# A decoder trunk on one core: Q/K outputs in three steps, class copies of K ahead of the exponentials, and stores and loads on other queues

## The chip, the core and the metric

The kernel runs on one core of a Trainium2 chip. The core has a matrix engine (TensorE, PE in the profile, with its weight loads as PEld), a vector engine (VectorE, DVE), a scalar engine (ScalarE, ACT), GpSimd (POOL) and a sync engine (SyncE, SP) that here only issues transfers. DVE, ACT, POOL and SP each work through their own instructions in the order of the program, so an instruction that waits holds up all that stands behind it on its engine. Transfers can be issued by SP, ACT and POOL; the issuing engine waits first for what the transfer needs. Sums of matmuls land in eight banks of PSUM. The metric is the device time of one execution in microseconds, as the median of several runs.

## What is computed

A two-layer decoder trunk over 1024 positions with a residual stream of width 1024, in float32. Layer 0 mixes with a short gated convolution, layer 1 with dilated attention; a SwiGLU network follows each. The change touches the attention layer alone. Its mixer, cut to what matters:

```
qkv = (h @ w_qkv).reshape(bsz, seq, 3, 16, 64)
for window, dilation in ((128, 1), (512, 4), (2048, 16)):
    # query t attends to keys t - j*dilation, j = 0..window//dilation
    s   = q.k / 8 + rel_bias[t5_bucket(distance)]     # masked outside the band
    lse = logsumexp(s);  o = exp(s - lse) @ v
alpha = softmax over the three branches of lse
o = sum(alpha * o) ;  x = x + o.reshape(seq, 1024) @ w_out
```

So a head's result is one weighted sum over all keys of its three branches, divided by one common sum of exponentials.

## The kernel before

All matrix products are made of float32 parts: an operand is split into a rounded high part, copied by ACT (line 141), and the low rest, subtracted by DVE (line 142), and each product is three matmuls (high by high, high by low, low by high). Large products use Strassen's scheme with seven products for a 2x2 block. The order of everything is written out by hand as Python generators that are stepped in turn; each step issues a few instructions, and the order of issue is the order on each engine.

**The Q/K phase.** `QueryKey.mix` (line 1142) makes Q and K of the first six pairs of heads: 42 products in `products` (588), each with `whole` (602), which may save a bank to SBUF on ACT (566, tile `part`) and add others on DVE (570). Each finished quarter of an output goes to `out`, which queues a generator in `waiting`. After each product `filled` calls `idle`, which steps that queue. One output (`emit`, 1124) is scaled by DVE (1128 for K, which also reorders it in time, 1130 for Q), split into high and low parts (tiles `kq_hi` and `kq_lo`), and both are stored to DRAM on POOL's queue (1135, 1136). Pairs 6 and 7 are made later by `projections` (1462) as filler in the attention.

**The attention.** Sixteen heads, two to a pair, p = n // 2 and a = n % 2. `slot(n)` (1710) issues the period of head n, in two loops of eight.

The first loop makes the logits of head n (`scores`, 1531) and the value products of head n - 1 (`values`, 1610) by turns. The logits of the branch with dilation 4 use `kca`, a copy of K ordered by residue class that ACT makes (`classes`, 1524, line 1528); the others use `ka` as loaded. DVE adds the bias (1555, 1564, 1581, 1586) and takes the maximum over the branches (up to 1595); POOL takes it over the partitions (1598, the all-reduce). At the end of the values ACT copies the numerators `o` and the denominators `z` out of PSUM (1640, 1641).

The second loop issues the softmax: five subtractions on DVE (1606), each followed by its exponential on ACT (1607), for the tiles `lf`, `lh`, `ld`, `lp` (two pieces); then, in its steps 5 and 6, the class copies of the next head.

Both loops also step the filler, `fill` (1802): the values V of later heads (`value_tiles`, 1478: lines 1489 to 1491, eviction 1494 on ACT, four stores to `vdram` per tile, 1498 on SP's queue), Q and K of pairs 6 and 7, and from head 12 on the first part of the output projection. A period has 15 steps of it (20 from head 13); a step is mostly six matmuls of 128x256 or three of 128x512. Without `late` the first loop takes one at its steps 0, 2, 4 and 6, and a period of an even head one more ahead of its logits; the second loop spreads what is left. Weights for the filler are loaded on SP (155) and split when `take` asks for the one ahead.

Transfers of a period: at its start bias, K and Q of the next head, on SP (1439, 1440 and 1518 to 1522); in even periods, between the loops, V of the pair into `vx` (`load_values`, 1501: six loads on ACT's queue, 1506 and 1508, which wait until PE has finished the pair before). Even periods also `finish` the pair before (1644): `z` is stored to DRAM (1649), loaded back as a thin tile `zc` (1652), inverted by DVE (1654), stored (1655) and loaded again as a broadcast over the partitions (1657), all four on SP's queue. The next odd period multiplies `o` by it on DVE (1704) and stores the result on POOL's queue (1705). For the last pair this runs on POOL's queue (1665, 1667, 1693, 1695).

Of the kernel before, what the change touches and what calls it, by code (L numbers as in the profile page):

```python
# [97 lines left out]
def trunk(ctx: ExitStack, tc: tile.TileContext, x, gains_in, cwi, ck, cwo, wqkv, wo, relb,  # L98
# [19 lines left out]
    def half(h):  # L118
        return slice(h * HALF, (h + 1) * HALF)
# [990 lines left out]
    class QueryKey(Conv):  # L1110


        def __init__(self, norm):
            Strassen.__init__(self, QK, norm, QK_PAIRS, 0, 1, 0, None)
            self.waiting, self.ready = [], False
            self.kq = {(p, part): dram.tile([256, S], F32, name=f"kq{p}_{part}")
                       for p in range(NPAIR) for part in range(2)}

# [5 lines left out]
        def emit(self, p, part, h, v):  # L1124

            t, rstd = half_page("kq"), self.norm.rstd[:, half(h)]
            if part == 1:
                nc.vector.tensor_tensor(out=by_time(t), in0=by_residue(v), in1=by_residue(rstd), op=ALU.mult)
            else:
                nc.vector.scalar_tensor_tensor(t, v, 0.125, rstd, op0=ALU.mult, op1=ALU.mult)  # L1130
            yield 1
            to = self.kq[p, part]
            hi, lo = half_page("kq_hi", F32R), half_page("kq_lo", F32R)
            split(t, (hi, lo))
            nc.gpsimd.dma_start(to[:128, half(h)], hi.bitcast(F32))
            nc.gpsimd.dma_start(to[128:, half(h)], lo.bitcast(F32))
            yield 1

        def work(self, u, c, v):
            yield from self.emit(u, 1 - c[0], c[1], v)  # L1140

        def mix(self):
            norm = self.norm
            prep = self.differences()
            stats = norm.stats(0, S)
            x12 = []

            def start(n):
                if n == 0:
                    next(prep)  # L1150
                    ensure(self.at(2, 2))
                elif n == 1:
                    next(prep)
                elif n == 3:
                    self.first(0)
                    ensure(self.at(4, 1))
                elif n == 4:
                    self.first(1)
                    ensure(self.at(4, 2))
                elif n == 5:  # L1160
                    ensure(self.at(0, 6))
                elif n == 6:
                    ensure(self.at(1, 6))
                elif n == 7:
                    next(prep)
                elif n == 8:
                    self.first(2)
                    ensure(self.at(0, 7))
                elif n == 9:
                    next(prep)  # L1170
                    next(prep)
                elif n in (10, 12):
                    next(prep)
                elif n == 11:
                    next(prep)
                    self.first(3)
                elif n == 13:
                    self.first(4)
                elif n == 14:
                    next(prep, None)  # L1180
                elif n == 20:
                    self.ahead = 3

            def gather():
                next(stats)

            def spread():
                run(stats)
                self.ready = True

            def load():
                for k in range(4):
                    x12.append(half_page("x12"))
                    nc.sync.dma_start(x12[k], spill[k][:, half(1)])

            def last_operand():
                self.b[8] = [None] * 4
                for k in range(4):
                    self.operand(8, k, k, x12[k])

            def filled(n):
                start(n)
                self.idle(n)

            norm.flush()
            self.base = op_state[1]
            ensure(self.at(0, 2))
            self.products(filled, {(1, 2): gather, (3, 1): spread, (5, 1): load, (5, 7): last_operand})
            self.h = [[self.b[1 + 7 * h * (k < 4) + (1 + h) * (k > 3)][k % 4] for k in range(KT)] for h in range(2)]
            self.step(None)  # L1210


    class Swiglu(Strassen):
# [239 lines left out]
    def attention(norm, qk):  # L1453
# [7 lines left out]

        def projections(p):

            late = []
            for part in (1, 0):
                w = take(("qkv", p, part), 2 - part)
                for h in range(2):
                    b = bank()
                    for _ in product(w, range(KT), qk.h[h], {HALVES[0]: b}):
                        if late and next(late[0], None) is None:  # L1470
                            late.pop()
                        yield
                    late.append(qk.emit(p, part, h, b))
                    next(late[0])
                    yield
            run(*late)

        def value_tiles(g, j):

            if j == 0:  # L1480
                wv[:] = [take(("v", g, i), 1) for i in range(2)]
            v = page("v")
            for b4 in range(4):
                t = 4 * j + b4
                b = bank()[:, :256]
                for k in range(KT):
                    (hi, lo), (whi, wlo) = qk.h[j][k], wv[k // 4]
                    a, c = slice(b4 * 128, b4 * 128 + 128), slice(k % 4 * 256, k % 4 * 256 + 256)
                    nc.tensor.matmul(b, hi[:, a], whi[:, c], start=k == 0, stop=False)  # L1489
                    nc.tensor.matmul(b, hi[:, a], wlo[:, c], start=False, stop=False)  # L1490
                    nc.tensor.matmul(b, lo[:, a], whi[:, c], start=False, stop=k == KT - 1)
                    if k % 2:
                        yield
                nc.scalar.activation(v[:, b4 * 256:b4 * 256 + 256], b, AF.Identity, scale=norm.r[:, t:t + 1])
                yield
            vd = vdram[g]
            for r in range(4):
                nc.sync.dma_start(bass.AP(vd.tensor, vd.offset + (512 * j + r) * 256,
                                          [[16 * 256, 32], [4 * 256, 4], [1, 256]]), v[32 * r:32 * r + 32])

        def load_values(p):
            src = vdram[p // 2]
            for a in range(2):
                off = src.offset + p % 2 * 128 + a * 64
                dims = slice(128 * a, 128 * a + 64)
                nc.scalar.dma_start(vx[:, 0:8, dims], bass.AP(src.tensor, off, [[256, 128], [128 * 256, 8], [1, 64]]))
                for h in range(2):
                    nc.scalar.dma_start(vx[:, 8 + 4 * h:12 + 4 * h, dims],
                                        bass.AP(src.tensor, off + 512 * 256 * h, [[1024, 128], [256, 4], [1, 64]]))

        def load_kq(n):
# [132 lines left out]
        def finish(p):  # L1644

            o, z = OZ.pop(p)
            if p < NPAIR - 1:
                zd, rd = zdram[p]
                nc.sync.dma_start(zd, z[0:65:64])
                yield  # L1650
                zc = scope["pool"].tile([128, 16], F32, name="zc", tag="zc", bufs=2)
                nc.sync.dma_start(zc, bass.AP(zd.tensor, zd.offset, [[16, 128], [1, 16]]))
                yield
                nc.vector.reciprocal(zc, zc)
                nc.sync.dma_start(bass.AP(rd.tensor, rd.offset, [[16, 128], [1, 16]]), zc)
                yield
                nc.sync.dma_start(z, bass.AP(rd.tensor, rd.offset, [[S, 2], [0, 64], [1, S]]))
                yield
                put_off.append((p, o, z))
                return  # L1660
# [49 lines left out]
        def slot(n, dense, ndense, late=0, hook=iter(())):  # L1710
# [28 lines left out]
            for i in range(8):  # L1739
                next(sc, None)  # L1740
                next(pv, None)
                next(pv, None)
                if i >= late and i % 2 == 0:
                    other(1)
                    used += 1
            run(sc)
# [8 lines left out]
            for i in range(8):  # L1755
                if a == 1 and i == 2:
                    attended()
                if i < FIN0 or i > SOFT:
                    next(extra, None)
                if i > SOFT:  # L1760
                    next(later, None)
                if i == SOFT:
                    if n < H:
                        live[n] = new
                        run(softmax(new))
                if i >= SOFT:
                    next(hook, None)
                other(left * (i + 1) // 8 - left * i // 8)
# [258 lines left out]
```

## Time and profile before

| | us |
|---|---|
| runs | 2250.13, 2250.79, 2255.63 |
| median | 2250.79 |
| profiled execution | 2252.32 |
| its span, first to last instruction | 2250.5 |
| mean granted PE clock | 0.976 |

The profile is of one execution. A row of a group gives line, engine and operation, tiles written and read, count, busy time and mean duration, and then the idle time of the engine just before and what ended it. A row of a stretch gives its limits, its length, and per engine the busy time and the count of instructions, and last the mean granted PE clock, the mean busy share of the 16 DMA engines and GB/s. A wait's releaser is inferred: where several things were waited for, it is the last. Matmuls overlap, so that the starts of two tell more than the duration of one.

### The profile page before, as it was taken

The page shows a single profiled execution, that of the slowest core. Times are in us where ns is not written, and L with a number is a line of the kernel's source. Part 1 is how long each engine was busy: PE and PEld are TensorE (multiplying, and loading weights), DVE is VectorE, ACT ScalarE, POOL GpSimd, SP SyncE. Part 2 cuts the span into 40 slices and gives each one's busy share as a digit, 9 for nine tenths or more (in the row PEclk, how much of TensorE's full clock was granted, in tenths as well). Part 3 has the DMA queues.
Part 4 walks back from the last instruction along what each step waited for, and adds up shares of the span by engine and source line. Part 5 has one row for each costly group of instructions (what it writes and reads, how often), then busy time and mean ns, then how long its engine had stood idle before and what let it go on. Part 6 is the DMA issues. An engine that isn't in the chain of part 4 may idle for free. (4 is left out here: it accounts for less than half of the span.)

```text
span 2250.5 us, 30931 instructions
## 1 busy us (share of the span) xinstructions
PE 2143.5 (95%) x11086; PEld 1834.9 (82%) x11086; DVE 1752.9 (78%) x3272; ACT 1004.3 (45%) x1848; POOL 219.1 (10%) x303
## 2 busy tenths in 40 slices
PE   9999999999999999998978888789999999999998
PEld 7888888888888888776877878678788888888887
DVE  8897679988887889688645564677898888888886
ACT  7333345444444644353333333344644444446435
POOL 1000000110100000002211111111101010101000
PEclk9999999999999999999998899899999999999999
DMA  7222652233333674416465554765422333357532
GB/s 217 89 87 78 213 159 70 89 111 105 107 108 123 201 215 131 148 64 205 171 150 144 132 151 120 206 177 165 112 94 99 104 108 104 108 190 219 174 97 75
DMA packets 147588, 304.91 MB, mean 135 GB/s; under 512 B 50328, under 2 KB 61608, under 8 KB 147434
## 3 DMA queue, kind: packets, MB, share of 16 engines
q1 hardware_dynamic: 81514, 201.59, 29.8%
q0 software_dynamic: 24752, 78.25, 10.7%
q10 hardware_dynamic: 41168, 23.10, 3.4%
q8 instruction: 88, 1.44, 0.3%
q14 instruction: 66, 0.54, 0.1%
HBM read 212.48 MB, written 83.05 MB: 131 GB/s over the span
## 5 line engine op out<-in xcount | busy, mean ns | idle before, releaser
L560 PE MATMUL bank<-b,w 128*128 128x512 f32 x1952 | 766.0, 392 | 7.0 <-ACT part L566 5.3
L562 PE MATMUL bank<-b,w 128*128 128x512 f32 x1952 | 763.1, 391 | 8.9 <-DVE w L142 8.8
L561 PE MATMUL bank<-b,w 128*128 128x512 f32 x1952 | 763.0, 391 | 2.5 <-DVE b L553 2.2
L562 PEld LDWEIGHTS bank<-b,w 128*128 128x128 f32 x1952 | 367.8, 188 | 91.9 <-DVE w L142 15.3
L560 PEld LDWEIGHTS bank<-b,w 128*128 128x128 f32 x1952 | 367.8, 188 | 86.5 <-ACT part L566 6.9
L561 PEld LDWEIGHTS bank<-b,w 128*128 128x128 f32 x1952 | 368.1, 189 | 79.1 <-DVE b L553 3.1
L141 ACT ACTIVATE w<-combo 128x512 fp32r<-128x512 f32 (+2 forms) x488 | 248.9, 540 | 222.1 <-DVE combo L189 205.3
L142 DVE TENSOR_TENSOR w<-combo,w 128x512 fp32r<-128x512 f32 (+2 forms) x488 | 276.1, 579 | 38.0 <-ACT w L141 37.3
L566 ACT ACTIVATE part<-bank 128x512 f32<-128x512 f32 x186 | 110.7, 595 | 384.2 <-PE bank L562 382.3
L142 DVE TENSOR_TENSOR w<-raw,w 128x512 fp32r<-128x512 f32 (+2 forms) x334 | 182.1, 566 | 37.5 <-ACT w L141 37.5
L570 DVE TENSOR_TENSOR part<-part,bank 128x256 f32<-128x256 f32 (+1 forms) x366 | 170.4, 495 | 30.1 <-PE bank L562 16.7
L141 ACT ACTIVATE w<-raw 128x512 fp32r<-128x512 f32 (+2 forms) x334 | 161.2, 525 | 47.6 <-PE bank L562 11.5
L369 PE MATMUL bank<-w_hi,w 128*128 128x512 f32 (+1 forms) x320 | 119.6, 374 | 0.0
L371 PE MATMUL bank<-w_hi,w 128*128 128x512 f32 (+1 forms) x320 | 117.9, 368 | 0.7 <-DVE w L142 0.7
L370 PE MATMUL bank<-w_lo,w 128*128 128x512 f32 (+1 forms) x320 | 117.8, 368 | 0.0
L790 DVE TENSOR_TENSOR x<-x,bank 128x512 f32<-128x512 f32 x136 | 92.5, 680 | 29.2 <-PE bank L562 29.2
L491 DVE TENSOR_TENSOR x<-x,bank 128x512 f32<-128x512 f32 (+1 forms) x104 | 66.3, 642 | 62.4 <-PE bank L371 58.3
L189 DVE TENSOR_TENSOR combo<-raw 128x512 f32<-128x512 f32 (+1 forms) x172 | 111.1, 646 | 0.0
L1544 PE MATMUL bank<-qa,kca 128*128 128x256 f32 (+1 forms) x128 | 40.9, 343 | 60.7 <-ACT kca L1528 60.7
L553 DVE TENSOR_TENSOR b<-hin,b 128x512 fp32r<-128x512 f32 x126 | 79.5, 683 | 9.3 <-ACT b L552 9.0
L1489 PE MATMUL bank<-w_hi,b 128*128 128x256 f32 x256 | 78.4, 306 | 7.6 <-ACT w_hi L141 7.6
L1555 DVE TENSOR_TENSOR lf<-bank,bias 128x256 f32<-128x256 f32 x64 | 24.0, 418 | 77.2 <-PE bank L1545 63.8
(248 smaller groups left out, 3716.3 us busy)
## 6 DMA issues: line engine op xcount, KB each, us to landing
hin<-part SPq DMA_DIRECT2D x126, 256.0 KB
raw<-in_ffn_w_gate SPq DMA_DIRECT2D x44, 512.0 KB
raw<-in_ffn_w_up SPq DMA_DIRECT2D x44, 512.0 KB
part<-sum POOLq DMA_DIRECT2D x72, 256.0 KB, 2.3
raw<-in_ffn_w_down SPq DMA_DIRECT2D x48, 384.0 KB
raw<-in_attn_w_qkv SPq DMA_DIRECT2D x27, 512.0 KB
raw<-in_conv_w_in SPq DMA_DIRECT2D x24, 512.0 KB
part<-part POOLq DMA_DIRECT2D x36, 256.0 KB, 2.4
```

Of the source, the lines that this page charges most:

```text
L141: nc.scalar.activation(hi, src, AF.Copy)
L142: eng.tensor_tensor(out=lo, in0=src, in1=hi, op=ALU.subtract)
L189: eng.tensor_tensor(out=c, in0=a, in1=b, op=op)
L369: nc.tensor.matmul(b, whi[:, a], ahi[:, s], start=first, stop=False)
L370: nc.tensor.matmul(b, whi[:, a], alo[:, s], start=False, stop=False)
L371: nc.tensor.matmul(b, wlo[:, a], ahi[:, s], start=False, stop=last)
L560: nc.tensor.matmul(b, hi[:, a], bhi, start=start and k == 0, stop=False, skip_group_check=True)
L561: nc.tensor.matmul(b, hi[:, a], blo, start=False, stop=False, skip_group_check=True)
L562: nc.tensor.matmul(b, lo[:, a], bhi, start=False, stop=k == n - 1, skip_group_check=True)
L566: nc.scalar.activation(t, b, AF.Copy)
L570: nc.vector.tensor_tensor(out=t, in0=t, in1=b, op=ALU.add)
L790: nc.vector.tensor_tensor(out=X[n][:, half(h)], in0=X[n][:, half(h)], in1=b, op=ALU.add)
```

## The change

- `emit` is in three steps instead of two: DVE scales; ACT copies the high part, which is stored; DVE subtracts the low part, which is stored. `step` now keeps two outputs going: after a product it issues the copy of the output before, the scaling of a new one, and the subtraction of the output before. In `projections` the steps of an output follow one per filler step.
- The class copies of the next head move from steps 5 and 6 of the second loop to steps 1 and 2, ahead of the softmax in step 4.
- The filler of the first loop keeps its steps 0 and 2 and gives up 4 and 6 (except with `late`, head 14); they go to the second loop.
- The four stores of a V tile move from SP's queue to ACT's, the six loads of `vx` from ACT's to SP's.
- The four transfers of `finish` move from SP's queue to POOL's (the last pair is unchanged).

```diff
-            yield 1
-            to = self.kq[p, part]
-            hi, lo = half_page("kq_hi", F32R), half_page("kq_lo", F32R)
-            split(t, (hi, lo))
+            yield
+            hi, lo, to = half_page("kq_hi", F32R), half_page("kq_lo", F32R), self.kq[p, part]
+            nc.scalar.activation(hi, t, AF.Copy)
             nc.gpsimd.dma_start(to[:128, half(h)], hi.bitcast(F32))
+            yield
+            nc.vector.tensor_tensor(out=lo, in0=t, in1=hi, op=ALU.subtract)
             nc.gpsimd.dma_start(to[128:, half(h)], lo.bitcast(F32))
-            yield 1
-
-        def work(self, u, c, v):
-            yield from self.emit(u, 1 - c[0], c[1], v)
+
+        def out(self, u, c, v):
+            self.waiting.append(self.emit(u, 1 - c[0], c[1], v))
+
+        def step(self, n):
+
+            for _ in range(n):
+                last, self.begun = self.begun, self.waiting.pop(0) if self.waiting else iter(())
+                next(last, None)
+                next(self.begun, None)
+                next(last, None)
+
+        def idle(self, n):
+            if self.ready:
+                self.step(1)
...
-            self.step(None)
+            self.step(len(self.waiting) + 1)
...
-            late = []
+            late = iter(())
...
-                        if late and next(late[0], None) is None:
-                            late.pop()
+                        next(late, None)
                         yield
-                    late.append(qk.emit(p, part, h, b))
-                    next(late[0])
+                    late = qk.emit(p, part, h, b)
+                    next(late)
                     yield
-            run(*late)
+            run(late)
...
-                nc.sync.dma_start(bass.AP(vd.tensor, vd.offset + (512 * j + r) * 256,
+                nc.scalar.dma_start(bass.AP(vd.tensor, vd.offset + (512 * j + r) * 256,
...
-                nc.scalar.dma_start(vx[:, 0:8, dims], bass.AP(src.tensor, off, [[256, 128], [128 * 256, 8], [1, 64]]))
+                nc.sync.dma_start(vx[:, 0:8, dims], bass.AP(src.tensor, off, [[256, 128], [128 * 256, 8], [1, 64]]))
                 for h in range(2):
-                    nc.scalar.dma_start(vx[:, 8 + 4 * h:12 + 4 * h, dims],
+                    nc.sync.dma_start(vx[:, 8 + 4 * h:12 + 4 * h, dims],
...
-                nc.sync.dma_start(zd, z[0:65:64])
+                nc.gpsimd.dma_start(zd, z[0:65:64])
...
-                nc.sync.dma_start(zc, bass.AP(zd.tensor, zd.offset, [[16, 128], [1, 16]]))
+                nc.gpsimd.dma_start(zc, bass.AP(zd.tensor, zd.offset, [[16, 128], [1, 16]]))
...
-                nc.sync.dma_start(bass.AP(rd.tensor, rd.offset, [[16, 128], [1, 16]]), zc)
+                nc.gpsimd.dma_start(bass.AP(rd.tensor, rd.offset, [[16, 128], [1, 16]]), zc)
...
-                nc.sync.dma_start(z, bass.AP(rd.tensor, rd.offset, [[S, 2], [0, 64], [1, S]]))
+                nc.gpsimd.dma_start(z, bass.AP(rd.tensor, rd.offset, [[S, 2], [0, 64], [1, S]]))
...
-                if i >= late and i % 2 == 0:
+                if (i >= late if late else i < 3) and i % 2 == 0:
                     other(1)
...
-                if i > SOFT:
+                if i in (1, 2):
                     next(later, None)
```

More of the change, by code (lines that the diff above doesn't have):

```diff
@@ L1114, in __init__ @@
             Strassen.__init__(self, QK, norm, QK_PAIRS, 0, 1, 0, None)
-            self.waiting, self.ready = [], False
+            self.waiting, self.ready, self.begun = [], False, iter(())
             self.kq = {(p, part): dram.tile([256, S], F32, name=f"kq{p}_{part}")
```

## The prediction

> **What bounds the kernel now.** I read the page first, for the engine that is busy throughout and for where its clock falls.
>
> ```profile
> span 2250.5 us, 30931 instructions
> PE 2143.5 (95%) x11086; PEld 1834.9 (82%) x11086; DVE 1752.9 (78%) x3272; ACT 1004.3 (45%) x1848; POOL 219.1 (10%) x303
> PEclk9999999999999999999998899899999999999999
> L1544 PE MATMUL bank<-qa,kca 128*128 128x256 f32 (+1 forms) x128 | 40.9, 343 | 60.7 <-ACT kca L1528 60.7
> ```
>
> TensorE (PE) bounds the whole: it is busy 95% of the span, and the digits of its granted clock dip only in one stretch, the attention. One line stands before most of PE's idle time there: logits that wait for kca, the class copy of K that ACT makes. Then I read two stretches, the Q/K phase and heads 1 to 12 (a head's period runs from its first logits to the next head's), and for the latter the list of PE's waits (us in total, times, longest):
>
> ```profile
> core 0: us, PE busy (x) PEld busy (x) DVE busy (x) ACT busy (x) POOL busy (x), PEclk, DMA share, GB/s
> 1000.00:1113.00 113.00, 100.99 (x430) 79.30 (x429) 92.28 (x137) 49.08 (x85) 24.88 (x46) 0.97 0.51 177
> 1155.90:1473.00 317.10, 256.27 (x1738) 242.12 (x1739) 178.62 (x316) 122.36 (x177) 51.18 (x33) 0.87 0.54 141
> ```
>
> ```profile
> PE bank L1544 <- ACT kca L1528: 56.4, 11, 9.4
> PE bank L1489 <- ACT w_hi L141: 6.3, 1, 6.3
> PE bank L369 <- ACT w_hi L141: 5.7, 1, 5.7
> ```
>
> Twelve heads take 317.1 us, 26.4 each; PE idles 60.8 of them. The waits' 56.4 include the 9.4 that end at 1155.9, so 47.0 lie inside. Each wait also leaves PE at half clock afterwards; the stretches from each restart to the clock's return (first, last and sum of 13):
>
> ```profile
> 1155.94:1160.80 4.86, 4.86 (x22) 4.86 (x23) 0.76 (x2) 1.32 (x2) 0.00 (x0) 0.50 0.39 100
> ...
> 1466.72:1473.00 6.28, 5.14 (x10) 2.72 (x11) 5.53 (x7) 6.28 (x7) 0.77 (x2) 0.50 0.31 91
> sum 65.73, PE 63.90 PEld 60.07 DVE 22.78 ACT 25.65 POOL 4.57; mean PE 4.92 PEld 4.62 DVE 1.75 ACT 1.97 POOL 0.35
> ```
>
> 63.9 us of work at half speed cost 32. So the work at full clock is 256.3 - 32 = 224.3 us, 18.7 a head. Last, the timeline of one even head (4), to see what a period's end waits for. Columns are start, duration, engine and line; the bracket is idle time and who ended it.
>
> ```profile
> 1248.70 0.69 DVE L1595 TENSOR_TENSOR m<-m,lp 128x512 f32<-128x512 f32 x1
> 1249.00 0.59 ACT L1641 ACTIVATE o<-bank 64x512 f32<-64x512 f32 x1
> 1249.60 3.22 POOL L1598 PARTITION_ALL_REDUCE mb<-m  x1 [21.84 <-ACT o L1641]
> 1251.78 0.28 PE L1489 MATMUL bank<-w_hi,b 128*128 128x256 f32 x1
> 1252.35 0.47 ACT L1494 ACTIVATE v<-bank,r 128x256 f32<-128x256 f32 x1 [2.76 <-DMA vx<-vdram]
> 1252.85 1.23 DVE L1606 TENSOR_TENSOR lf<-lf,mb 128x1024 f32<-128x1024 f32 x1 [3.46 <-POOL mb L1598]
> 1253.82 0.28 PE L1491 MATMUL bank<-w_hi,b 128*128 128x256 f32 x1
> 1254.11 1.06 ACT L1607 ACTIVATE lf<-lf 128x1024 f32<-128x1024 f32 x1 [1.28 <-DVE lf L1606]
> 1256.80 0.25 DVE L1654 RECIPROCAL zc<-zc 128x16 f32<-128x16 f32 x1
> 1256.81 1.02 ACT L1607 ACTIVATE lp<-lp 128x384 f32<-128x384 f32 x2
> 1257.74 2.10 ACT L1528 ACTIVATE kca<-ka 128x512 fp32r<-128x512 f32 x2
> 1258.88 0.58 PE L1544 MATMUL bank<-qa,kca 128*128 128x256 f32 x1 [4.78 <-ACT kca L1528]
> ```
>
> Count from the end of the maximum, M = 1249.39. The filler ends at M+4.7 and kca's first half at M+9.4, only because it stands behind five exponentials that it does not need. The first exponential, which the next values need, ends at M+5.8.
>
> **The change part by part.**
>
> Class copies first. ACT is free from M+0.2 to M+4.7 (2.76 of that it spends on loads that move away); the copies' 2.10 fit under the all-reduce's 3.22. The 47.0 go and, where no other long wait comes, the 32. What the copies now wait for is K's landing, and the exponentials are queued behind them: if that cover goes, values slip with K. The program issues K's loads at the start of the same period, some 12 us before.
>
> Filler. Two steps move behind the logits. From 1251.78 to 1253.82 PE starts 18 matmuls, 0.12 each; a step has six, 0.7. The filler of head 4 then ends at M+6.1, and the values want the first exponential after four logit matmuls, at M+6.6: it is there 0.8 earlier. For an odd head:
>
> ```profile
> 1273.38 0.69 DVE L1595 TENSOR_TENSOR m<-m,lp 128x512 f32<-128x512 f32 x1
> 1284.35 0.58 PE L1544 MATMUL bank<-qa,kca 128*128 128x256 f32 x1 [3.78 <-ACT kca L1528]
> ```
>
> Head 5's filler ends 6.5 after its maximum (1284.35 - 3.78 against 1274.07). With the two steps, the one that stands ahead of an even head's logits (0.7) and the four matmuls (0.5) that is 9.1: a slack of 3.3. Nothing is added to PE's work, so the move itself costs nothing while DVE follows. But DVE has 178.62/12 = 14.9 us a head against 18.7, and with the 3.4 for which it waits on the all-reduce that is 18.3: nearly a second bound. I add 0.5 a head, **6**, between 0 and the 2 a head at which a head would take DVE's sum and its weight splits one after the other (24).
>
> Two waits for weights stay: their splits stand behind the exponentials in ACT's order before and after.
>
> ```profile
> 1204.54 1.99 ACT L141 ACTIVATE w_hi<-raw 128x1024 fp32r<-128x1024 f32 x2
> 1132.23 2.49 SPq L1498 DMA_DIRECT2D vdram<-v  x4
> ```
>
> Head 2's 6.3 loses 1.4 to the longer filler and gains the four V stores, 2.5, now ahead of the split on ACT: 7.5. Head 12's 5.7 falls to about 4.5 for the filler. With the low parts (1) and 2.5 of clock each: **18** kept.
>
> V stores on ACT, V loads on SP. A V tile puts 2.49 of issues on ACT; six tiles end in these heads. Where one ends before the exponentials with a split behind it (heads 5 and 10), DVE's low part waits, and the subtractions behind that: 2 us each, 1 at head 6: **5**. Bounds: 0 if ACT's gap takes them all, 6 x 2.5 = 15. ACT loses the six V loads, on which it stood idle 2.76 at head 4. On SP they wait for PE's last values of the pair, and raw weights and the next head's bias, K and Q loads stand behind them, with most of a head's time to go: I count nothing, at worst those 2.8 at six heads (17) if the loads come due at once.
>
> The reciprocal's chain on POOL. Stores and loads of the denominators now wait behind the all-reduce. The broadcast of one pair on SP and who waits for it; the stretch in which nothing else moved (its last two columns are DMA share and GB/s); the last pair's chain, which runs on POOL already:
>
> ```profile
> 1209.61 0.54 SPq L1657 DMA_DIRECT2D z<-rdram  x1
> 1225.66 1.22 DVE L1704 TENSOR_TENSOR o<-o,z 128x1024 f32<-128x1024 f32 x1 [1.93 <-DMA z<-rdram]
> ```
>
> ```profile
> 1221.00:1224.00 3.00, 3.00 (x28) 3.00 (x28) 2.15 (x5) 1.26 (x3) 0.11 (x1) 1.00 0.13 52
> ```
>
> ```profile
> 1556.92 0.55 POOL L1665 DMA_DIRECT2D zdram<-z  x1 [14.87 <-ACT z L1640]
> 1559.80 0.59 POOL L1667 DMA_DIRECT2D zl<-zdram  x1 [2.33 <-DMA zdram<-z]
> 1564.02 0.54 POOL L1693 DMA_DIRECT2D rdram<-zl  x1 [3.63 <-DVE zl L1692]
> 1568.95 1.06 POOL L1695 DMA_DIRECT2D z<-rdram  x2 [4.40 <-DMA rdram<-zl]
> ```
>
> From issue to issue the last pair takes 2.9, 4.2 (of which I take 3, the rest being work of its own) and 4.9 us. From M+3.5 the broadcast z so goes out at M+14 (M+12 if its source is written as fast as the first 2.9). It took 16.0 on SP, at a DMA share of 0.13, two engines of sixteen, once alone: 512 KB at 52 GB/s are 10. So it lands between M+22 and M+30; I take the middle, M+26. The next (odd) head's maximum comes at M+19, its all-reduce ends at M+22.4, so o x z (1.22) must start by M+21.2, or the subtractions queued behind it on DVE slip: by 4.8, which less the slack of 3.3 is 1.5, at six odd heads **9**. Bounds: 0 (landing M+24) and 6 x (5.5 + 2.5 clock) = 48 (M+30). The next head's all-reduce comes to POOL at M+19.2, five after the chain's last issue, so it isn't held up. DVE's reciprocal also waits for zc, about 1.5 us, with the next head's evictions behind it; their slack is in the 6 above.
>
> By the Trainium skill (DMA: Bandwidth & Descriptors, Issuing engines are not separate DMA queues) a transfer gains nothing from another queue, as all run on the same engines; the 0.13 agrees, and by it the move is worth SP's issue time alone.
>
> By the Trainium skill (TensorE: Matmul & The Clock Gate, Why this matters for your kernels) idle gaps under about 3 us do not cost the clock. The trace has 0.50 after waits of 4.8 and more; if gaps of 1.5 cost it too, the sum would be 15 us higher.
>
> Head 0: the exponentials, not kca, end its 9.4 wait.
>
> ```profile
> 1151.08 1.06 ACT L1607 ACTIVATE lf<-lf 128x1024 f32<-128x1024 f32 x1
> ```
>
> That is 3.8 before 1155.9; the V stores ahead of the very first copy cost up to 2.5: **-2.3**. Head 13 and the start hold the other 4.3 us of kca waits: **-3.6** with clock.
>
> Q/K phase.
>
> ```profile
> ACT kq_hi L141 <- DVE kq L1130: 22.6, 10, 3.5
> PE bank L560 <- ACT part L566: 5.3, 2, 3.0
> PE bank L562 <- DVE w L142: 3.9, 5, 1.4
> ```
>
> ACT's copy waits for the scaling just issued, and PE for a save queued behind that copy. A product apart, the copy waits for nothing. In the projections between the heads the steps move by one filler step, which changes no order that PE waits for. Of 12.0 idle (113 - 101) 9.2 are these two; no instruction is added. I take **-7**, between 0 (DVE, 82% busy, makes the weights late anyway) and -12.
>
> Sum: 224.3 + 18 + 6 + 5 + 9 = 262.3 against 317.1, so -54.8; with -2.3, -3.6 and -7 it is **-67.7**. The profiled execution took 2252.32 us, its span of 2250.5 and 1.8 around it, which leaves it at 2252.3 - 67.7 = 2184.6; it lies 1.5 over the median of the runs, 2250.79, so I forecast **2183**.
>
> **The rivals.**
>
> z late on POOL. It lands at M+28.5: gaps of 4.0 and 2.5 of clock at six heads are 39 instead of 9: **2213**. For: 16.0 on SP. Against: on SP it shared a ring with a head's loads.
>
> All is hidden: z spreads or lands by M+24, ACT's gap takes the stores, 9 + 5 less: **2169**. By the Trainium skill (DMA: Bandwidth & Descriptors, Why a DMA increments its semaphore by 16 and not by 1) the software path gives some copies all 16 engines; no run here shows it for a broadcast.
>
> Slower. The z wait takes over at every odd head. Seven pairs must give back 67.7 + 9 = 77, 11 each, 8.5 of wait and 2.5 of clock: it decides from a landing at M+33 on (21.2 + 3.3 + 8.5), 19 after the issue. At 20, M+34, seven waits of 9.5 + 2.5 are 84 in place of 9: **2258**. For: it has the slowest load of the stage behind three landings and an all-reduce. Against: 16.0 is what it took with a whole head's loads behind it.
>
> It does not do what it says: K lands so late that the copies end where they did. If half of the 47 and of the 32 remain, 40: **2223**. For: the first half of kca now wants K some 8 us sooner after the logits. Against: the program issues K's loads at the start of the period, ahead of its logits, and SP gets rid of the chain with its waits on ACT and DVE.
>
> **How the numbers follow.** Forecast 0.48, z late 0.22, all hidden 0.16, slower 0.08, K late 0.06. Range 2156 to 2226: the lower end is the hidden case with DVE's 6 and the other 5 of the Q/K phase, the upper one z late with 13 of the bounds for V stores and loads; slower is left out. Faster 0.89, same 0.03 (edges of the last two), slower 0.08; 0.3% is about what this kernel's runs can tell from none.
>
> **What would show it.** Right: no PE wait on kca in heads 1 to 13; PEclk of the twelve heads over 0.95; periods near 21 to 22; the waits for w_hi at heads 2 and 12 still there; DVE's o x z waiting on z by some 5 us; no PE wait on part in the Q/K phase. Wrong: PE waiting for exponentials at most heads; ACT's kca waiting for ka; the all-reduce waiting behind POOL's chain; periods of odd heads near 25.

## The result, and the profile after

| | runs | median us | lowest to highest | ratio to before, 95% interval |
|---|---|---|---|---|
| before | 4 | 2252.18 | 2250.13 to 2255.63 | 1 |
| after | 4 | 2225.59 | 2221.55 to 2227.41 | 0.9878, 0.9858 to 0.9898 |

The change makes the kernel 27 us faster; 68 were forecast. M is, as in the prediction, the end of a head's maximum. The lines of the changed kernel stand 11 lower in the attention, so that 1528 became 1539, 1544 1555, 1607 1618, 1617 1628 and 1704 1715. First the page of after, then three of its stretches (length, then busy time of PE, PEld, DVE, ACT and POOL with counts, granted clock, DMA share and GB/s): the end of the Q/K phase, head 0, and heads 1 to 12.

```profile
span 2224.7 us, 30938 instructions
PE 2125.2 (96%) x11086; PEld 1823.8 (82%) x11086; DVE 1747.7 (79%) x3272; ACT 1007.3 (45%) x1848; POOL 234.5 (11%) x331
PEclk9999999999999999999999888899999999999999
L1628 PE MATMUL bank<-lf,vx 128*128 128x128 f32 x256 | 43.3, 324 | 53.4 <-ACT lf L1618 53.4
```

```profile
1000.00:1113.00 113.00, 112.46 (x583) 96.03 (x582) 91.38 (x139) 54.33 (x93) 27.68 (x50) 1.00 0.61 205
1118.00:1132.50 14.50, 14.23 (x104) 13.97 (x105) 9.95 (x20) 6.64 (x7) 2.40 (x1) 0.86 0.83 218
1132.50:1450.80 318.30, 244.42 (x1740) 231.31 (x1740) 180.74 (x321) 126.15 (x182) 63.39 (x55) 0.87 0.58 149
```

The twelve heads, where 54.8 us were to come from, take 318.3 us against 317.1 before. Nearly all of the gain lies ahead of them: head 0 starts at 1118.0 (before 1133.3, 15.3 later), and its period is 14.5 long instead of 22.6, 8.1 less. Heads 13 to 15 and what follows bring another 3.6; with that the spans differ by 25.8 (15.3 + 8.1 - 1.2 + 3.6).

The list of waits of after in the twelve heads (us in total, times, longest) says what took the place of the waits on kca: PE first, then DVE.

```profile
PE bank L1628 <- ACT lf L1618: 53.4, 7, 14.9
PE bank L1500 <- ACT w_hi L141: 8.6, 1, 8.6
PE bank L369 <- ACT w_hi L141: 5.0, 1, 5.0
...
DVE o L1715 <- DMA z<-rdram: 55.5, 5, 16.0
DVE zc L1665 <- DMA zc<-zdram: 26.0, 6, 5.6
```

No wait on kca is left there. PE now waits 53.4 us for the first exponential of a head (`lf`), more than the 47.0 that went, and DVE waits 55.5 us for the broadcast z. The timeline shows that these are one chain. From the maximum of head 4 (M = 1217.43) to the values that follow head 5:

```profile
1216.74 0.69 DVE L1606 TENSOR_TENSOR m<-m,lp 128x512 f32<-128x512 f32 x1
1220.71 0.56 POOL L1660 DMA_DIRECT2D zdram<-z  x1
1226.52 0.57 POOL L1663 DMA_DIRECT2D zc<-zdram  x1 [5.25 <-DMA zdram<-z]
1230.20 0.54 POOL L1666 DMA_DIRECT2D rdram<-zc  x1 [3.11 <-DVE zc L1665]
1233.38 0.82 POOL L1668 DMA_DIRECT2D z<-rdram  x1 [2.65 <-PE bank L1556]
1237.89 3.22 POOL L1609 PARTITION_ALL_REDUCE mb<-m  x1 [3.69 <-DVE m L1606]
1253.28 1.23 DVE L1715 TENSOR_TENSOR o<-o,z 128x1024 f32<-128x1024 f32 x1 [15.57 <-DMA z<-rdram]
1255.56 1.22 DVE L1617 TENSOR_TENSOR lf<-lf,mb 128x1024 f32<-128x1024 f32 x1
1256.81 1.06 ACT L1618 ACTIVATE lf<-lf 128x1024 f32<-128x1024 f32 x1 [16.30 <-DVE lf L1617]
1257.91 0.79 PE L1628 MATMUL bank<-lf,vx 128*128 128x128 f32 x2 [14.95 <-ACT lf L1618]
```

The broadcast is issued at M+16.0 and DVE's product with it starts at M+35.9. The all-reduce of head 5 is done at 1241.11, but its subtraction stands behind that product on DVE and starts at 1255.56; so the exponential, the values and PE come 15 us late. The clock is lost as well: after the restart PE works 4 us at half speed. This happens three times, with waits of 14.95, 14.53 and 14.24 us at heads 6, 8 and 10, which are 43.7 of the 53.4.

### The profile page after: what moved, and what is told of

It is laid out like the page before. It is cut to its first block, busy times and chain, and to the rows that moved or that the text cites. A ratio compares the mean times of both kernels' runs of the same rounds, so it can differ in the third digit from the quotient of the medians.

```text
span 2224.7 us, 30938 instructions
## 1 busy us (share of the span) xinstructions
PE 2125.2 (96%) x11086; PEld 1823.8 (82%) x11086; DVE 1747.7 (79%) x3272; ACT 1007.3 (45%) x1848; POOL 234.5 (11%) x331
## 4 chain that ended last, share of the span: by engine, by line
PE 82%; DVE 7%; DMA 6%; issue 3%; ACT 2%; POOL 1%; SPq 0%; ACTq 0%; DVEq 0%; POOLq 0%
PE bank L562 19%; PE bank L561 18%; PE bank L560 18%; DMA z<-rdram 3%; PE bank L1628 3%; PE bank L371 3%; PE bank L370 3%; PE bank L369 3%; PE bank L652 3%; PE bank L655 3%; PE bank L654 3%; DVE w L142 1%; PE bank L1556 1%; DVE b L553 1%; PE bank L1501 1%
## 5 line engine op out<-in xcount | busy, mean ns | idle before, releaser
L142 DVE TENSOR_TENSOR w<-raw,w 128x512 fp32r<-128x512 f32 (+2 forms) x334 | 183.0, 569 | 35.9 <-ACT w L141 35.9
L1628 PE MATMUL bank<-lf,vx 128*128 128x128 f32 x256 | 43.3, 324 | 53.4 <-ACT lf L1618 53.4
L1628 PEld LDWEIGHTS bank<-lf,vx 128*128 128x128 f32 x256 | 39.9, 236 | 55.2 <-ACT lf L1618 54.9
```

What stands on the lines that cost most here:

```text
L142: eng.tensor_tensor(out=lo, in0=src, in1=hi, op=ALU.subtract)
L1628: nc.tensor.matmul(view(acc[ih], off, dims), vx[:, u, 64 * a:64 * a + 128], rhs, start=first, stop=last)
```

## The experiments

Theories. **Narrow**: the broadcast is slow because it runs on two of the 16 DMA engines and shares them with the loads of the next head, from whichever queue it is issued. **Queue**: it is slow because it was moved to POOL. Later runs price the other parts. "Twelve heads" is the time from the first logits of head 1 to those of head 13 in the profiled execution.

| run | kernel | median us | ratio, 95% interval | twelve heads |
|---|---|---|---|---|
| | before | | 1 | 317.1 |
| | after | 2225.59 | 0.9878, 0.9858 to 0.9898 | 318.3 |
| e1 | after, chain of the denominators on SP | 2214.69 | 0.9840, 0.9824 to 0.9857 | 298.2 |
| e2 | after, wide broadcast, on POOL | 2177.64 | 0.9678, 0.9656 to 0.9699 | 269.5 |
| h2 | after, wide broadcast, chain on SP | 2173.45 | 0.9657, 0.9639 to 0.9675 | 262.7 |
| e3 | before, Q/K outputs in three steps alone | 2233.70 | 0.9922, 0.9903 to 0.9941 | 316.2 |
| e4 | before, class copies ahead alone | 2238.92 | 0.9948, 0.9932 to 0.9965 | 303.9 |
| f1 | before, wide broadcast alone | 2250.82 | 0.9990, 0.9976 to 1.0004 | 316.5 |
| h1 | before, class copies and wide broadcast | 2198.55 | 0.9770, 0.9754 to 0.9786 | 269.1 |
| f2 | e2, V stores and loads back | 2186.24 | 0.9711, 0.9689 to 0.9734 | 275.6 |
| f3 | e2, filler back | 2182.73 | 0.9693, 0.9674 to 0.9713 | 274.1 |
| g1 | e2, weights of V further ahead | 2167.37 | 0.9626, 0.9605 to 0.9646 | 262.2 |
| g2 | g1, chain on SP | 2157.44 | 0.9580, 0.9566 to 0.9595 | 251.0 |

Before was measured again beside each group of runs; the differences below are made from the ratios, 0.001 being 2.25 us.

### The queue or the width of the broadcast

e1 puts the four transfers of `finish` back on SP:

```diff
-                nc.gpsimd.dma_start(zd, z[0:65:64])
+                nc.sync.dma_start(zd, z[0:65:64])
...
-                nc.gpsimd.dma_start(z, bass.AP(rd.tensor, rd.offset, [[S, 2], [0, 64], [1, S]]))
+                nc.sync.dma_start(z, bass.AP(rd.tensor, rd.offset, [[S, 2], [0, 64], [1, S]]))
```

> The changed kernel with the four transfers of finish back on SP's queue. Theory N (the broadcast is narrow: on two of sixteen engines it takes 13 to 21 us to land, wherever it is issued): the chain starts some 5 us earlier, but z still takes about 16 us; it lands near M+25 to M+29, DVE's o x z still waits 3 to 8 us at several odd heads and PE keeps waits of 1 to 5 us for lf; 2185 to 2205 us. Theory Q (POOL's queue is to blame: start behind the all-reduce, small transfers that land in 5.5 instead of 2.3 us): no PE wait for lf is left, 2165 to 2175 us.

e2 leaves them on POOL and issues the broadcast as two transfers, one for each head of the pair:

```diff
-                nc.gpsimd.dma_start(z, bass.AP(rd.tensor, rd.offset, [[S, 2], [0, 64], [1, S]]))
+                for a in range(2):
+                    nc.gpsimd.dma_start(z[64 * a:64 * a + 64], bass.AP(rd.tensor, rd.offset + a * S, [[0, 64], [1, S]]))
```

> The changed kernel with the broadcast of z as two transfers of 64 partitions each (64 outermost, so that it can spread), still on POOL's queue at the end of the same chain. Theory N: each half lands 3 to 5 us after its issue, near M+21; DVE's waits for z fall from 55 us to under 10, the PE waits of 15 us for lf go; 2165 to 2178 us. Theory Q: the chain on POOL is still late by its start and its small transfers, DVE keeps more than half of its waits; over 2195 us.

e2 gains 45 us on after, e1 only 8.6. The same bytes on the same queue are enough: the timeline of e2 at the place shown above, the landings of the broadcast in after and in e2 (pieces, size of one, median us from issue to landing), and PE's wait in e2 (11.8 us instead of 53.4):

```profile
1233.25 1.04 POOL L1669 DMA_DIRECT2D z<-rdram  x2 [2.35 <-PE bank L1556]
1238.03 3.22 POOL L1609 PARTITION_ALL_REDUCE mb<-m  x1 [3.74 <-DVE m L1606]
1238.04 2.95 DVE L1716 TENSOR_TENSOR o<-o,z 128x1024 f32<-128x1024 f32 x1 [0.19 <-DMA z<-rdram]
1244.41 1.16 PE L1628 MATMUL bank<-lf,vx 128*128 128x128 f32 x8 [1.56 <-ACT lf L1618]
```

```profile
z<-rdram POOLq DMA_DIRECT2D x5, 512.0 KB, 19.8
...
zdram<-z POOLq DMA_DIRECT2D x6, 8.0 KB, 5.6
```

```profile
z<-rdram POOLq DMA_DIRECT2D x10, 256.0 KB, 4.1
```

```profile
PE bank L1628 <- ACT lf L1618: 11.8, 7, 2.7
```

The issue is at the same moment to 0.13 us; the broadcast lands in 4.1 us instead of 19.8, the product is done before the subtraction is due, and the long waits are gone.

How many engines it used shows in the rows of the DMA queues: packets, MB, and the packets' time as a share of 16 engines. By their bytes, q0 carries POOL's transfers, q1 SP's and q10 ACT's. From 1236 to 1237 us in after (first row) and from 1235 to 1236 us in e2 (second row) nothing moved but z:

```profile
q0 software_dynamic: 15, 0.04, 13.7%
...
q0 software_dynamic: 93, 0.32, 103.3%
```

13.7% of sixteen engines are 2.2 of them; 103.3% are all (a packet is counted where it starts). In after the two are shared as well. From 1237 to 1240 us, with the engines busy for 65% of the time in all, z still moved 0.16 MB, 53 GB/s (first row); from 1241 to 1244 us, when the transfers of SP and ACT filled them, it moved 0.07 MB, under half:

```profile
q0 software_dynamic: 39, 0.16, 13.4%
...
q1 hardware_dynamic: 216, 0.55, 58.4%
q10 hardware_dynamic: 333, 0.31, 37.9%
q0 software_dynamic: 18, 0.07, 8.2%
```

The Trainium skill (DMA: Bandwidth & Descriptors, Why a DMA increments its semaphore by 16 and not by 1) says that the number of engines follows from the slowest dimension on each side of the transfer, as the largest number up to 16 that divides both: here two for a leading [S, 2], sixteen for 64 partitions. The 13.7% and 103.3% agree; the exception that it names for POOL's path, on which the rival "all is hidden" leaned, did not show here.

e1 missed what was expected of it by either theory. In its profiled execution the twelve heads are 20.1 us shorter than in after, and what follows them is 7.8 longer, so that less reaches the total. On SP the narrow broadcast is late too, and it does a second harm: the Q loads behind it on that queue land late. PE's longest waits in e1, and the landings of the Q loads there, in after, where the same narrow broadcast runs on POOL, and in e2:

```profile
PE bank L1555 <- DMA qa<-kq: 16.7, 3, 6.1
PE bank L1628 <- ACT lf L1618: 11.8, 6, 5.1
```

```profile
qa<-kq SPq DMA_DIRECT2D x22, 256.0 KB, 16.4
...
qa<-kq SPq DMA_DIRECT2D x22, 256.0 KB, 6.2
...
qa<-kq SPq DMA_DIRECT2D x28, 256.0 KB, 5.9
```

h2 then takes both, the wide broadcast and SP (the diffs of e1 and e2 together):

> The changed kernel with the wide broadcast and all four transfers of the denominators on SP instead of POOL. The same with the wide broadcast on POOL gave 2177.6. If the queue is indifferent once the broadcast runs on all engines: 2173 to 2182. If POOL is the slower queue for the small transfers (5.3 to 6.8 us against 2.3 for the first store): below 2172. If the chain's waits on SP hold up the loads behind them: above 2183, with PE waiting for qa.

2173.45 against e2's 2177.64, with intervals that overlap: here the queue matters far less than the width. (With the weights' wait gone too, the same move is worth 10 us: g2 below.) Its twelve heads:

```profile
1133.20:1395.90 262.70, 235.66 (x1740) 223.15 (x1739) 181.69 (x321) 126.59 (x182) 52.57 (x34) 0.95 0.67 172
```

The prediction's sum for these heads was 262.3, its granted clock over 0.95. PE's longest waits there in h2:

```profile
PE bank L1628 <- ACT lf L1618: 8.8, 4, 3.1
PE bank L1500 <- ACT w_hi L141: 8.6, 1, 8.6
PE bank L369 <- ACT w_hi L141: 5.0, 1, 5.0
```

So this kernel, whose broadcast lands in time, comes to the predicted length, though in part because errors of other terms cancel (see below); the two waits for weights that the sum kept are there, and one of 8.8 us in all for exponentials.

### Single parts on the kernel before

e3 has the three steps of an output alone (the first half of the change's diff, up to `run(late)`); e4 has the copies alone:

```diff
-                if i > SOFT:
+                if i in (1, 2):
                     next(later, None)
```

> The kernel before with the three-step outputs alone (Q/K phase and projections). The trace of after has 112.5 of 113 us busy there against 101.0: if that is the three steps' own doing the time falls by 14 to 18 us, to 2234 to 2238, with nothing changed in the attention. If part of it came from the moved queues, or if the prediction's 7 was right, 2243 to 2246.

> The kernel before with the class copies alone moved to steps 1 and 2 of the second loop; the chain stays on SP, the filler where it was. Theory N: the waits for kca (60.7 us) go, but in shorter periods the broadcast on SP is late too: DVE's o x z waits for z at most odd heads and PE for lf; about half the gain of 80 is kept, 2205 to 2225 us. Theory Q: with the chain on SP there is no wait for z; 2180 to 2195 us.

e3 gains 17.6 us, all of it ahead of head 0 (1114.1 instead of 1133.3). In the stretch from 1000 to 1113 us and in the list of PE's waits around it:

```profile
1000.00:1113.00 113.00, 112.02 (x581) 95.56 (x579) 90.84 (x139) 54.74 (x94) 27.68 (x50) 1.00 0.61 201
```

```profile
PE bank L1555 <- ACT kca L1539: 11.5, 2, 9.9
...
PE bank L562 <- DVE w L142: 0.4, 1, 0.4
```

The wait on ACT's save is gone, and the one on DVE's weights, which the prediction let stand, fell from 3.9 to 0.4. DVE's own waits for the copies `kq_hi` fell from 16.8 us to 2.2 in the stretch.

e4 keeps 12 us, where the copies were to remove 47 of waits alone; it missed both ranges above. What PE and DVE wait for is of the kind seen in e1, the Q loads and z:

```profile
PE bank L1544 <- DMA qa<-kq: 23.7, 5, 6.3
PE bank L1617 <- ACT lf L1607: 17.8, 8, 5.5
...
DVE o L1704 <- DMA z<-rdram: 24.5, 5, 8.0
```

f1 and h1 settle it: the wide broadcast on the kernel before without and with e4's edit, on SP.

```diff
-                nc.sync.dma_start(z, bass.AP(rd.tensor, rd.offset, [[S, 2], [0, 64], [1, S]]))
+                for a in range(2):
+                    nc.sync.dma_start(z[64 * a:64 * a + 64], bass.AP(rd.tensor, rd.offset + a * S, [[0, 64], [1, S]]))
```

> The kernel before with nothing changed but the broadcast of z, as two transfers of 64 partitions on SP's queue. Theory N: before, the narrow broadcast was hidden behind the waits for kca (DVE waited 4.8 us for it in all), so spreading it is worth nothing by itself: 2246 to 2252 us. Rival: it already held up K, Q and weights behind it on SP; 2240 us or less.

> The kernel before with two edits alone: class copies of K at steps 1 and 2, and the broadcast of z as two transfers of 64 partitions, still on SP. The copies alone gave 2238.9, the wide broadcast alone 2250.8 of 2252.2. If the narrow broadcast is what kept the copies from paying, by its own landing and by the Q loads held up behind it on SP, this run gains most of the 47 us of waits on kca: 2195 to 2210, with the PE waits on qa gone and DVE's waits on z under 2 us at most. If loads on ACT, the filler's place or the denominators' wait hold the periods in any case: 2225 to 2240.

The wide broadcast alone is worth nothing that can be told (0.9990, up to 1.0004), as PE still waits 58.2 us for kca there and the twelve heads keep their length; the copies alone are worth 12 us; both together 52, and PE no longer waits for Q. Its two longest waits in these heads of h1, for the first exponential and for weights:

```profile
PE bank L1617 <- ACT lf L1607: 13.0, 6, 5.3
PE bank L369 <- ACT w_hi L141: 10.5, 1, 10.5
```

### The V transfers and the filler, priced on e2

f2 undoes the move of the V stores and loads, f3 that of the filler:

```diff
-                nc.scalar.dma_start(bass.AP(vd.tensor, vd.offset + (512 * j + r) * 256,
+                nc.sync.dma_start(bass.AP(vd.tensor, vd.offset + (512 * j + r) * 256,
...
-                nc.sync.dma_start(vx[:, 0:8, dims], bass.AP(src.tensor, off, [[256, 128], [128 * 256, 8], [1, 64]]))
+                nc.scalar.dma_start(vx[:, 0:8, dims], bass.AP(src.tensor, off, [[256, 128], [128 * 256, 8], [1, 64]]))
...
```

```diff
-                if (i >= late if late else i < 3) and i % 2 == 0:
+                if i >= late and i % 2 == 0:
```

> The version with the wide broadcast on POOL (2177.6 us), with V's stores back on SP and V's loads back on ACT. By the prediction's terms the stores on ACT cost 2.5 at head 2, 3 at the start and 5 at heads 5, 6 and 10, and the loads' 2.8 a pair that ACT loses are hidden: 2165 to 2175 us. Rival: with V's loads on ACT, ahead of the class copies and exponentials of even heads, those come 3 to 4 us late and PE waits for lf; 2185 to 2200 us.

> The version with the wide broadcast on POOL (2177.6 us), with the four filler steps back between the logits. By the prediction the filler then ends 1.4 us earlier against the exponentials, and PE, which waits up to 2.7 us for lf at seven heads now, waits about 1.4 more at those and one or two at others: 15 to 20 us more with some clock, 2188 to 2198 us. Rival: the values find the exponential ready either way, as the logits end later too; 2175 to 2181 us.

The V move is worth 7 us, at the edge of what the intervals tell apart. ACT's list of waits in f2 shows why it can be a gain, by the rival named above: with the loads on ACT, the copies that now come first stand behind loads that wait for PE.

```profile
ACT kca L1539 <- DMA vx<-vdram: 20.9, 5, 5.5
```

The filler's move is worth 3 us by the ratios, which can't be told from nothing; f3's 2182.73 lies between the two ranges expected.

### A faster version

What still stops PE in e2 is the wait for V's weights at head 2 (8.6, the row of line 1500 in after) and the start, where V's stores stand ahead of the first copy on ACT. g1 splits the second weight of a group one step sooner and puts the first group's V stores on SP; g2 also puts the chain on SP, as in h2.

```diff
-                wv[:] = [take(("v", g, i), 1) for i in range(2)]
+                wv[:] = [take(("v", g, i), 1 + i) for i in range(2)]
...
-                nc.scalar.dma_start(bass.AP(vd.tensor, vd.offset + (512 * j + r) * 256,
+                (nc.scalar if g else nc.sync).dma_start(bass.AP(vd.tensor, vd.offset + (512 * j + r) * 256,
```

> The version with the wide broadcast on POOL (2177.6 us), with both weight halves of the next V group split one group ahead (head 2's wait of 8.6 us with its half clock), and the stores of the very first V group on SP (4.6 us wait for kca at the start). Both waits stand in no cover: 8.6 + 0.7 + 3 of clock and 3 + 1: 2160 to 2166 us. Rival: the split only moves, in front of other exponentials; 2172 to 2180 us.

> The kernel of g1 (wide broadcast, weights of the values split one head earlier, first group's V stores on SP) with the four transfers of the denominators on SP instead of POOL. With the wide broadcast alone the two queues gave 2173.5 (SP) and 2177.6 (POOL). If POOL's slower small transfers (DVE waits 27 us for zc there, under 1 on SP) are worth something on their own: 2160 to 2165 against g1's 2167.4. If the waits that g1 removed had been hiding SP's own (the chain on SP stands ahead of bias, K and Q loads): 2168 to 2178, with PE waiting for qa or kca.

g1 gains 12 us on e2, a little less than expected, and g2 another 10, a little more: 2157.44, or 95 under before. The intervals of g1 and g2 do not overlap, so here the queue of the chain counts. PE's two longest waits in g2 from 960 to 1560 us:

```profile
PE bank L1628 <- ACT lf L1618: 8.2, 5, 2.6
PE bank L369 <- ACT w_hi L141: 4.9, 1, 4.9
```

## Why the prediction was right and wrong

**Right: the sign, the copies and the waits for weights.** The waits on kca went from the heads, and PE's lost time with them wherever the next wait was short: h1 shows 48 us in the twelve heads from copies and a wide broadcast alone (317.1 to 269.1). The waits for weights stayed where they were put: 8.6 and 5.0 against 7.5 and 4.5.

**Wrong: the term for z, 9 us.** The step that failed is "So it lands between M+22 and M+30; I take the middle, M+26". At head 4 it was issued at M+16.0 and landed 19.8 us later, at M+35.8. Two things were off. The small transfers take longer on POOL: from issue to issue the steps are 5.8, 3.7 and 3.2 us, where 2.9, 3 and 4.9 were taken from the last pair; in all that is 2 us. And 16.0 us on SP was taken for the dear end of the landing's bounds, as if its own queue were all that slowed it; on POOL three landings took 19.8 to 21.0. The row with a DMA share of 0.13 already said that it has two engines; what was not drawn from it is that these two also carry their share of the other loads (0.16 MB of z in 3 us while the engines had time free, 0.07 once the others filled them). Against the term of 9 and its bound of 48 the price was 45 us by after against e2, and 50 with the chain on SP as well (after against h2, 0.9878 - 0.9657).

**The rivals.** The mechanism is the one of "slower", at its place: a z wait behind which the subtractions of an odd head are held, decisive from M+33 on. It was given a chance of 0.08 and all seven pairs. It struck three, the odd heads 5, 7 and 9, where z landed at M+35.8, M+39.6 and M+35.7, counted from the maximum of the even head before; the other four landed at M+30.2 to M+32.2, after 12.8 to 16.7 us. So the place was right, and the result, 2225.59, came to lie at the upper end of the range (2226), between "z late" and "slower", by a landing later than the one and rarer than the other. That it is inside at all is luck: 14 us more than forecast outside the twelve heads made up for a part of the 56 fewer in them. (The lower end, from the terms named for it, would be 2169 - 6 - 5 = 2158, not 2156; nothing hangs on it.)

**"The 0.13 agrees", on the queue.** That the move to POOL gains nothing came out, as a sentence beside a sum that it did not change; but the 0.13 was read on SP alone and could say nothing of another queue. The move is a loss: 8.6 us with the narrow broadcast (e1), 5 with the wide one, where the intervals overlap (h2), and 10 with the weights further ahead, where they do not (g2 against g1). The small transfers land later on POOL and start behind the all-reduce; which of the two costs more was not taken apart.

**Q/K phase, -7.** It gave 17.6 alone (e3), beyond the bound of 12. What failed is the reason for staying under 9.2, "DVE, 82% busy, makes the weights late anyway": DVE is as busy in e3, but its waits for copies that were not there yet fell from 16.8 us to 2.2, and its weights came in time as well. The bound itself left out the clock that the gaps cost (0.97 over 113 us, 3.4).

**Head 0, -2.3.** Measured -8.1. "The exponentials, not kca, end its 9.4 wait" was to say that with the copies ahead PE would stop for the first exponential next, 3.8 earlier. But head 1's logits need only the copies; the exponentials are wanted by the values a few matmuls later, and there PE waits 2.5. The start cost 3.1, not 2.5 at most: the wait on kca there is 4.64 after and 1.56 before, and 1.6 again in g1 and g2, whose first V stores are on SP.

**V transfers, +5, and the filler, +6.** For the stores only a cost was counted, and the loads' departure from ACT was noted and priced at nothing; f2 prices the pair at 7 us the other way, at the edge of its intervals, with 20.9 us of waits on ACT. For the filler the sum has 6 for DVE beside a move at no cost; f3 shows no such cost, and its 3 us the other way can't be told from nothing.

**By stage.** Outside the twelve heads 12.9 us were forecast and 27.0 came (25.8 of the span, and the 1.2 that the heads lost), 14 more. Inside, 54.8 were forecast and -1.2 came, 56 fewer; h2, which differs from after by the chain's shape and queue alone, is 55.6 shorter there. The difference of the two is the 42 us by which the forecast missed. By f2 the V move came out some 12 better than its term, and in h2 DVE does not wait for z, for which the sum has 9; as its heads still take 262.7, other terms of that sum must be dearer. So its agreement with 262.3 is in part luck; which terms they are was not taken apart.

## What to carry to other kernels

When a long wait goes, list what the next instruction in each queue waits for and when it lands under the load of a shorter period; a transfer that was hidden by the old wait is the first suspect, and its landing beside traffic, not alone, is its price. Read the DMA share of a transfer that moves alone, and check in the rows of the queues that nothing else did: 0.13 means two engines of sixteen, and then its shape is worth changing before its queue. A part can be worth nothing alone and 40 us beside another, so price parts both ways, added to the kernel before and taken from the one after.

## What the runs showed of the hardware

- The same 512 KB broadcast from POOL took 12.8 to 21.0 us as one transfer with a leading dimension of two, and 4.1 us (median) as two transfers of 64 partitions. As one transfer on SP it also held up the loads behind it: Q landed after 16.4 us in e1, after 6.2 in after, where the broadcast ran on POOL, and after 5.9 in e2.
- Transfers of 8 KB landed later from POOL under this load: 5.6 us for the first store (the row above). The load behind it waited 30.7 us at six pairs on POOL in after, and 10.3 at seven on SP in e1.
- A gap of 2.53 us cost the clock. In after, at head 1, the gap and what followed it:

```profile
1133.19:1135.72 2.53, 0.00 (x1) 0.00 (x1) 2.37 (x3) 1.11 (x2) 0.13 (x1) 1.00 1.02 232
1135.70:1139.10 3.40, 3.38 (x16) 3.38 (x17) 2.35 (x5) 3.20 (x6) 0.00 (x0) 0.50 0.66 153
```

  The Trainium skill (TensorE: Matmul & The Clock Gate, Why this matters for your kernels) puts the limit at about 3 us; here the measurement lies below it. The gap of 1.56 in e2, shown above, was followed by full clock. The length alone does not decide: a gap of 2.16 in e2 was followed by half clock (0.50 from 1327.5 to 1330.6), one of 2.69 in before by full clock (1.00 from 1500.1 to 1503.5). What else does was not tested.
- DVE's product that began with POOL's all-reduce took 2.95 us (e2, 1238.04), against 1.23 in after, where the all-reduce was long done. No run was made on this.
